# A fixed order on TensorE for both attentions of an encoder layer: the second turned and multiplied in pairs of key chunks, the first with other places for scores and v tiles

## The chip, the cores and the metric

The kernel runs on one core of one Trainium2 chip. A core has a matrix engine (TensorE, PE in the profile; its weight loads are PEld), three engines for element-wise work (VectorE or DVE, ScalarE or ACT, GpSimd or POOL), a queue engine that issues most transfers (SyncE or SP), on-chip memory (SBUF), accumulation banks that PE writes (PSUM), and 16 DMA engines. Each engine runs its own instructions in order, and engines wait for each other through semaphores. The metric is the device time of one execution in microseconds, as the median of several runs.

## The reference

One layer of a bidirectional encoder over 2048 tokens of 1024 features, batch 1, all float32:

```python
h  = rms_norm(x, norm_mix[l])
z  = h @ w_in[l]             # q_A k_A v_A q_B k_B v_B gate_A gate_B
y_a = windowed_gqa(q_a, k_a, v_a, sink[l])        # |t-s| <= 128, ALiBi, 8 heads, 2 kv heads
y_b = neighborhood_attn(q_b, k_b, v_b, rpb[l])    # 8 heads, 32 x 64 grid, 8 x 16 neighbours
gates = sigmoid([g_a, g_b] + b_gate[l])
x  = x + (gates_a * (y_a @ w_proj_a[l]) + gates_b * (y_b @ w_proj_b[l])) @ w_out[l]
x  = x + square(relu(rms_norm(x) @ w_up[l])) @ w_down[l]
return rms_norm(x, norm_final)
```

The first attention (A) lets each token see the tokens within 128 places, with a linear bias by distance and a sink logit for each head. The second (B) puts the tokens on a grid of 32 rows by 64 columns; each sees a window of 8 rows by 16 columns, with a learned bias for each head and offset. Heads are 64 wide.

## The kernel before, in words

**Precision.** A large product is made of three matmuls of float32r halves (lines 203 to 205 of a helper `mm3`: high by high, high by low, low by high). An attention product uses two (probabilities split into a high part `ph` and a low part `pl`).

**Stages.** Input projections of the first token pages as block products (0 to 358 us of the span); attention A (358 to about 627); attention B (to about 1022); gates, projections and merge (to about 1340); the MLP's two products (to the end). Both attentions need little of PE and much of the other engines, so the rest of the input projection, "feature" tiles, is laid between their matmuls. `dense` lists these tiles: q, k and v of A and B, and 16 gate tiles, each for two pages of 512 tokens. `feature_steps` does one tile in 8 steps of three 512-column matmuls into a PSUM bank "mm" (two of them) and yields after each; `fill = chain(dense)` strings the tiles together. Weights of a tile arrive by DMA (`raw`), ACT rounds them (`whl`, L179, about 1 us) and DVE or POOL takes the low part (L180, 2.4 us on POOL). ACT and DVE take a finished tile out of "mm". A v tile is then transposed: ACT copies it to `z` (L737), PE turns that copy by four transposes (`v_parts`, L423), and ACT and DVE take the result out.

**Attention A.** 32 units of 128 query tokens by one kv head (4 query heads). `Unit.load` fetches the queries (qraw), `order` arranges them on POOL (qa, L797). `score(u)` makes one quarter's scores (two matmuls, L815) into one of three "s" banks; DVE adds the bias and takes the row maximum in the same instruction (`sa`, L819). After the fourth quarter comes the softmax: four exps on ACT (L826), sums and reciprocal on DVE (L827, L828), four scalings on POOL (L830). `turn(c)` transposes one chunk of 128 keys by four transposes (L837) into one of two "pt" banks, ACT copies it as `ph` (L841), DVE makes `pl` (L842). `product(c)` multiplies both by the values into the one "av" bank (L852, L853); after the unit's last chunk ACT copies one half out (`ya`, L859) and DVE adds the other (L860), and the sum goes to memory `y_a` over SP.

The order on PE is written out by hand here: under `in_turn()` each group is put behind the last one issued (`issued[0]`). For each of a unit's chunks (3; 2 at the ends of the sequence): the turn, scores of the unit three ahead (quarters 0, then 1 and 2, then 3 in the three chunks), feature steps by `plain(upto)`, which spreads 24 tiles (one page each) of 8 steps evenly over the chunks, and the product of the chunk before. Ahead of this loop the first three units' scores are given without a fixed order, and 20 feature steps with one.

**Attention B.** 32 units of 8 heads by 4 column bands (`attn_b`). Each fetches its queries (`qb`, three buffers) and values (`vb`), makes four score blocks (L1038; 288 to 512 columns) that DVE reduces with the unit's bias (`sb`, L1043), does the softmax (exps L1049 on ACT, L1051 on DVE, L1054 on POOL), and then, for four pairs of key chunks, transposes into "pt" (L1066), copies (`phb` L1071, `plb` L1072) and multiplies into "av" (L1078); at the end ACT and DVE take the sum out (`yb`, L1086, L1087). Bias tables are made on POOL (L1006) from a fetched table (`braw`, L1000) for 22 of the 32 units. Keys of a head (`kb`, 2 MB in three DMAs, L1015 to L1017) have two buffers. What PE does when is not written out here: the scheduler places a unit's instructions, `drive` gives units two ahead, and `paced` puts each remaining feature tile behind the last product of some unit (`done`), 20 tiles of the 44 left in one call and 24 in another.

**Queues.** Transfers share SP's queue in order; a transfer into memory that attention A used must wait until the last reader there is done.

Of the kernel before, what the change touches and what calls it, by code (L numbers as in the profile page):

```python
# [19 lines left out]
BH = 8  # L20
# [75 lines left out]
def encoder_layer(ctx, tc, x, norm_mix, w_in, b_gate, sink, rpb, w_pa, w_pb, w_out,  # L96
# [323 lines left out]
    def v_parts(col, b, vt, p2, v2):  # L420

        for t in range(4):
            PE.transpose(p2[:, t * P : (t + 1) * P], vt[:, t * P : (t + 1) * P], ident)  # L423
# [304 lines left out]
    def v_tile(col):  # L728
        raw = load_slice([(cols(w_in[0], col), KC)])
        yield  # L730
        hl = split_slice(raw, V if col == O_VA else G)
        yield
        for b in (2, 3):
            ps = psum("mm", 2)
            yield from feature_steps(ps, hl, hp[b])
            vt = T(wp, [P, 2, BT], F32, "z", 3)[:, 0]
            A.copy(vt, ps)  # L737
# [19 lines left out]
        G.tensor_scalar(t, t, slope[:, g : g + 1], 1.0, ALU.mult, ALU.mult)  # L757
        bias_a[g] = t

    done, began, shares = [], [], []  # L760
# [19 lines left out]
    def in_turn():  # L780
        return tc.issue_after(issued[0]) if issued[0] else nullcontext()
# [89 lines left out]
                next(gens[k + 1])  # L871
            yield from g

    def drive(units, live, last, ahead=2):

        for u in units:
            next(u)
            live.append(u)
            if len(live) > ahead:
                next(live.pop(0), None)  # L880
        while last and live:
            next(live.pop(0), None)

    def paced(filler, pieces, total, lag):

        for n in pieces:
            at = min(n * 32 // total - lag, 31)
            with tc.issue_after(done[at]) if at >= 0 else nullcontext():
                piece(filler)

    def piece(filler):
        while next(filler, None):
            pass

    def gate_tile(f, blocks):
        raw = load_slice([(cols(w_in[0], O_GA + f * P), KC)])
        yield
# [43 lines left out]
    given = 0  # L941

    def plain(upto):
        nonlocal given
        while given < upto:
            with in_turn():
                next(fill)
            given += 1

    plain(FIRST)  # L950
# [24 lines left out]
    flush(queue=SY)  # L975
    s_a.close()

# [39 lines left out]
        SY.dma_start(k[64:128, 1].bitcast(F32), kd[0:64])  # L1017
        return k

    def attn_b(n_u, h, j, k, bias):  # L1020
        e, t = h % 2, h // 2
        w, jt = B_W[j], JT[j]
        kp = 4 * w
        q = T(bp, [P, 4, P], F32R, f"qb{n_u % 3}", 1)
        SY.dma_start(q.bitcast(F32), qs_b[t][e][:, :, j])
        yield
        v = T(bp, [P, 8, P], F32R, f"vb{n_u % 3}", 1)
        SY.dma_start(v[: 4 * w].rearrange("p (b c) d -> p b (c d)", b=4).bitcast(F32),
                     vs_b[t][4 * B_C0[j] : 4 * (B_C0[j] + w), :, e * 256 : e * 256 + 256])
        st = T(bp, [P, 4, 4], F32, "stb", 8)  # L1030
        mx, nm, sm, ri = (st[:, n, :] for n in range(4))
        kv = k.rearrange("p z (q f) -> p z q f", q=8)
        s = []
        for i in range(4):
            n = B_NR[i] * w
            ps = psum("s", 3)
            for z in range(2):
                PE.matmul(ps[:, :n], q[:, i, :],  # L1038
                          kv[:, z, B_R0[i] // 4 : (B_R0[i] + B_NR[i]) // 4, 4 * B_C0[j] : 4 * (B_C0[j] + w)],
                          start=z == 0, stop=z == 1)  # L1040
            o = boff[(jt, IT[i])]
            si = T(bp, [P, 512], F32, f"sb{n_u % 3}", 4)
            V.tensor_tensor_reduce(out=si[:, :n], in0=ps[:, :n], in1=bias[:, o : o + n], scale=1.0, scalar=-3.0e38,  # L1043
                                   op0=ALU.add, op1=ALU.max, accum_out=mx[:, i : i + 1])
            s.append(si)
        A.activation(nm, mx, AF.Copy, scale=-0.125)
        for i in range(4):
            n = B_NR[i] * w
            last_exp[0] = A.activation(s[i][:, :n], s[i][:, :n], AF.Exp, bias=nm[:, i : i + 1], scale=0.125,  # L1049
                                       accum_out=sm[:, i : i + 1]).ins  # L1050
        V.reciprocal(ri, sm)  # L1051
        for i in range(4):
            n = B_NR[i] * w
            G.tensor_scalar(s[i][:, :n], s[i][:, :n], ri[:, i : i + 1], 1.0, ALU.mult, ALU.mult)  # L1054
        yield
        flush(queue=SY)
        po = psum("av", 1)
        first = True
        for pair in range(4):
            pt = psum("pt", 2)  # L1060
            at, pieces = 0, []
            for c in (2 * pair, 2 * pair + 1):
                i0, ni = B_USE[c]
                for i in range(i0, i0 + ni):
                    rr = (4 * c - B_R0[i]) * w
                    PE.transpose(pt[:kp, at + (i - i0) * P : at + (i - i0 + 1) * P], s[i][:, rr : rr + kp], ident)  # L1066
                pieces.append((c, i0, ni, at))
                at += ni * P
            ph = T(bp, [P, 512], F32R, "phb", 3)
            pl = T(bp, [P, 512], F32R, "plb", 3)  # L1070
            last_parts[0] = (A.copy(ph[:kp, :at], pt[:kp, :at]).ins,  # L1071
                             V.tensor_tensor(out=pl[:kp, :at], in0=pt[:kp, :at], in1=ph[:kp, :at].bitcast(F32),  # L1072
                                             op=ALU.subtract).ins)
            if pair == 0:
                pieces.reverse()
            for c, i0, ni, o in pieces:
                for z, src in enumerate((ph, pl)):
                    last = PE.matmul(po[:, i0 * P : (i0 + ni) * P], v[:kp, c, :],  # L1078
                              src[:kp, o : o + ni * P], start=first, stop=(c == 7 and z == 1),
                              skip_group_check=True).ins  # L1080
                    first = False
        done.append(last)

        at = n_u % 2 * 64
        y = yb[at : at + 64]
        A.copy(y, po[64 - at : 128 - at, :])  # L1086
        V.tensor_tensor(out=y, in0=po[at : at + 64, :], in1=y, op=ALU.add)  # L1087
        put(y_b[t].rearrange("(e d) (i j t) -> e d i j t", e=2, i=4, j=4)[e, :, :, j, :],
            y.rearrange("d (i t) -> d i t", i=4))

    def all_b():
        for h in range(BH):
            k = load_k(h)

            for n, j in enumerate((0, 3, 1, 2) if h == 0 else range(4)):
                if j != 2:
                    bias = make_bias_b(h, JT[j])
                u = attn_b(4 * h + n, h, j, k, bias)
                next(u)
                yield u  # L1100

    def ahead_of(units, n):
        ready = []
        for u in units:
            ready.append(u)
            if len(ready) > n:
                yield ready.pop(0)
        yield from ready
# [5 lines left out]
    flush(queue=SY)  # L1114
    drive(units, live, True)
    flush(queue=SY)
    s_b.close()
    s_pg = ExitStack()
# [25 lines left out]

    first_y = load_y(0)
    first_load = last_dma[0]
    paced(fill, range(20, 44), 38, 4)
    s_h.close()


# [596 lines left out]
```

## Time and profile before

| what | value |
|---|---|
| median of three runs | 2611.38 us (2610.45 to 2614.44) |
| the profiled execution's own time | 2610.25 us |
| its span, first to last instruction | 2608.4 us |
| PE busy between 336 and 358 us | 21.17 of 22.00 us |
| PE busy between 1022 and 1300 us | 278.00 of 278.00 us |
| mean granted clock of PE | 0.998 |

The span leaves out 1.85 us around the first and last instruction. A row of a timeline gives the start and the length of a group of like instructions, its engine, line, operation and tiles (out<-in), and in brackets the idle time ahead of it with what ended it. Matmuls are pipelined: a printed length of 0.39 us for a 512-column matmul holds some 0.16 of overlap with the next, so the distance between starts is what a matmul costs. Granted clock is the share of full speed at which PE was allowed to run.

### The profile page before, as it was taken

How to read it: one execution, taken by the hardware profiler on the slowest of the kernel's cores; microseconds unless marked ns; L12 is line 12 of the kernel's file. 1: busy time of each engine (PE TensorE's matmuls, PEld its weight loads, DVE VectorE, ACT ScalarE, POOL GpSimd, SP SyncE). 2: the span in 40 equal slices, each digit the busy share in tenths (PEclk: the TensorE clock that was granted, in tenths of full speed). 3: DMA queues.
4: the chain of work that ended last, by engine and by line, in shares of the span. 5: the costliest groups of instructions: out<-in, count | busy, mean ns of one | idle time of the engine just before them, and what ended most of it. 6: DMA issues, size and time to landing. Idle time of an engine off the chain costs nothing.

```text
span 2608.4 us, 34594 instructions
## 1 busy us (share of the span) xinstructions
PE 2572.6 (99%) x12140; PEld 2144.1 (82%) x12140; DVE 1610.4 (62%) x2621; ACT 1233.2 (47%) x2261; POOL 367.0 (14%) x493
## 2 busy tenths in 40 slices
PE   8999999999999999999999999999999999999999
PEld 6888878878888888888888888888888888888887
DVE  9866566665434444765478777766656535554766
ACT  5335347666545555543335544644444332323454
POOL 1000124454545541000000000100000000000010
PEclk9999999999999999999999999999999999999999
DMA  5657485467875745865465765854428825445555
GB/s 185 203 156 204 135 263 155 125 169 194 216 188 171 202 141 180 281 198 159 153 202 198 242 217 199 309 179 146 158 97 310 294 97 186 146 146 169 185 192 172
DMA packets 354127, 490.40 MB, mean 188 GB/s; under 512 B 28808, under 2 KB 188808, under 8 KB 351776
## 3 DMA queue, kind: packets, MB, share of 16 engines
q1 hardware_dynamic: 346896, 471.14, 57.8%
q10 hardware_dynamic: 7056, 17.04, 1.8%
q8 instruction: 96, 1.57, 0.3%
q14 instruction: 79, 0.65, 0.1%
HBM read 328.64 MB, written 159.45 MB: 187 GB/s over the span
## 4 chain that ended last, share of the span: by engine, by line
PE 90%; DVE 3%; DMA 3%; ACT 2%; issue 1%; SPq 0%; POOL 0%; POOLq 0%; DVEq 0%; ACTq 0%
PE b L311 15%; PE b L312 15%; PE b L313 15%; PE mm L203 6%; PE mm L205 6%; PE mm L204 6%; PE zb L313 3%; PE zb L311 3%; PE zb L312 3%; PE pt L203 2%; PE pt L204 2%; PE pt L205 2%; PE av L1078 2%; PE pt L1066 2%; PE s L1038 2%; PE pt L837 1%
## 5 line engine op out<-in xcount | busy, mean ns | idle before, releaser
L312 PE MATMUL b<-dwh,dah 128*128 128x512 f32 x896 | 348.6, 389 | 0.0
L313 PE MATMUL b<-dwh,dah 128*128 128x512 f32 x896 | 347.6, 389 | 0.0
L311 PE MATMUL b<-dwh,dah 128*128 128x512 f32 x896 | 339.6, 389 | 0.0
L307 ACT CAST dah<-da 128x1024 fp32r<-128x1024 f32 (+1 forms) x128 | 120.8, 945 | 368.8 <-PE b L313 240.5
L308 DVE TENSOR_TENSOR dah<-da,dah 128x1024 fp32r<-128x1024 f32 (+1 forms) x128 | 139.4, 1089 | 222.3 <-ACT dah L307 222.1
L312 PE MATMUL b<-ubh,uwhlb 128*128 128x512 f32 x592 | 230.3, 389 | 0.0
L311 PE MATMUL b<-ubh,uwhlb 128*128 128x512 f32 x592 | 230.3, 389 | 0.0
L313 PE MATMUL b<-ubh,uwhlb 128*128 128x512 f32 x592 | 229.2, 389 | 0.0
L203 PE MATMUL mm<-hT,whl 128*128 128x512 f32 x544 | 218.2, 401 | 0.0
L205 PE MATMUL mm<-hT,whl 128*128 128x512 f32 x544 | 215.1, 395 | 0.0
L204 PE MATMUL mm<-hT,whl 128*128 128x512 f32 x544 | 214.8, 395 | 0.0
L311 PEld LDWEIGHTS b<-dwh,dah 128*128 128x128 f32 x896 | 168.2, 188 | 34.9
L313 PEld LDWEIGHTS b<-dwh,dah 128*128 128x128 f32 x896 | 168.2, 188 | 34.9
L312 PEld LDWEIGHTS b<-dwh,dah 128*128 128x128 f32 x896 | 168.2, 188 | 34.8
L311 PE MATMUL zb<-zh,zwhl 128*128 128x512 f32 x476 | 186.4, 394 | 6.6 <-DVE st L251 1.6
L312 PE MATMUL zb<-zh,zwhl 128*128 128x512 f32 x476 | 186.3, 391 | 0.0
L313 PE MATMUL zb<-zh,zwhl 128*128 128x512 f32 x476 | 183.9, 392 | 0.3 <-DVE zwhl L308 0.3
L302 DVE TENSOR_TENSOR uc<-b,uc 128x512 f32<-128x512 f32 x160 | 108.9, 687 | 104.6 <-PE b L313 103.5
L1617 POOL TENSOR_TENSOR st<-st,power 128x1 f32<-128x1 f32 x16 | 13.3, 841 | 925.2 <-DVE st L1616 925.2
L311 PEld LDWEIGHTS b<-ubh,uwhlb 128*128 128x128 f32 x592 | 111.2, 188 | 23.4 <-issue 0.4
L312 PEld LDWEIGHTS b<-ubh,uwhlb 128*128 128x128 f32 x592 | 111.2, 188 | 23.1
L313 PEld LDWEIGHTS b<-ubh,uwhlb 128*128 128x128 f32 x592 | 111.1, 188 | 23.1
(255 smaller groups left out, 5840.0 us busy)
## 6 DMA issues: line engine op xcount, KB each, us to landing
at<-uc SPq DMA_DIRECT2D x224, 256.0 KB
da<-at SPq DMA_DIRECT2D x96, 512.0 KB
dw<-in_w_down_dram SPq DMA_DIRECT2D x160, 256.0 KB
uraw<-in_w_up_dram SPq DMA_DIRECT2D x32, 1024.0 KB
raw<-in_w_in_dram SPq DMA_DIRECT2D x34, 512.0 KB
zraw<-in_w_in_dram SPq DMA_DIRECT2D x16, 1024.0 KB
z<-zg SPq DMA_DIRECT2D x64, 256.0 KB
zg<-zc SPq DMA_DIRECT2D x32, 256.0 KB
```

The costliest lines, as they stand in the source:

```text
L203: PE.matmul(ps, lh, rh, start=first, stop=False)
L204: PE.matmul(ps, lh, rl, start=False, stop=False)
L205: return PE.matmul(ps, ll, rh, start=False, stop=last).ins
L302: return eng.tensor_tensor(out=out, in0=a, in1=b, op=op).ins
L307: casts.append(A.copy(hi, src).ins)
L308: return eng.tensor_tensor(out=lo, in0=src, in1=hi.bitcast(F32), op=ALU.subtract).ins
L311: PE.matmul(ps, lh, rh, start=first, stop=False, skip_group_check=True)
L312: PE.matmul(ps, lh, rl, start=False, stop=False, skip_group_check=True)
L313: PE.matmul(ps, ll, rh, start=False, stop=last, skip_group_check=True)
L1038: PE.matmul(ps[:, :n], q[:, i, :], kv[:, z, B_R0[i] // 4 : (B_R0[i] + B_NR[i]) // 4, 4 * B_C0[j] : 4 * (B_C0[j] + w)], start=z == 0, stop= ...
L1066: PE.transpose(pt[:kp, at + (i - i0) * P : at + (i - i0 + 1) * P], s[i][:, rr : rr + kp], ident)
L1078: last = PE.matmul(po[:, i0 * P : (i0 + ni) * P], v[:kp, c, :], src[:kp, o : o + ni * P], start=first, stop=(c == 7 and z == 1), skip_grou ...
```

## The change

Both attentions now run on PE in an order that the program fixes. Numbers of matmuls and their shapes stay the same on PE.

In A, the first three units' scores stand at set feature steps (`FIRST`: ahead of quarter 3 of unit 0 are 12 steps, and so on to 21), in order from that quarter on. The scores three units ahead are given as quarters 0 and 1, 2 and 3, none in a unit's three chunks. `plain` gets its numbers from weights (a score 0.27, a step 0.68) so that scores and steps together are even. A v tile yields "turn" after its copy, and its transposes are an owed step of their own, given ahead of the next feature step.

```diff
         for t in range(4):
-            PE.transpose(p2[:, t * P : (t + 1) * P], vt[:, t * P : (t + 1) * P], ident)
+            issued[0] = PE.transpose(p2[:, t * P : (t + 1) * P], vt[:, t * P : (t + 1) * P], ident).ins
         if col == O_VA:
...
+            yield "turn"
             out = v_parts(col, b, vt, psum("mm", 2), T(wp, [P, 2, BT], F32, "z", 3).rearrange("p a b -> p (a b)"))
             for dst, t in out:
                 SY.dma_start(dst, t)
@@ -757,7 +758,7 @@
...
-    AHEAD, FIRST, PLAIN = 3, 20, 24 * KC
+    AHEAD, PLAIN, SCORE, STEP = 3, 24 * KC, 0.27, 0.68
+    FIRST = {(0, 3): 12, (1, 2): 14, (2, 0): 16, (2, 2): 18, (3, 0): 21}
...
+    given, owed = 0, [False]
+
+    def plain(upto):
+        nonlocal given
+        while given < upto:
+            if owed[0]:
+                with in_turn():
+                    next(fill)
+            with in_turn():
+                owed[0] = next(fill) == "turn"
+            given += 1
 
...
     for n in range(AHEAD):
         prepare(n)
         for u in range(4):
-            units[n].score(u, False)
...
+                plain(FIRST[n, u])
+            units[n].score(u, (n, u) >= (0, 3))
+    plain(FIRST[AHEAD, 0])
     chunks = [(n, c) for n, x in enumerate(units) for c in range(x.c0, x.c1)]
-    behind = []
+    behind, scored, begin = [], 0, given
+    whole = (PLAIN - given) * STEP + 4 * (len(units) - AHEAD) * SCORE
...
         if n + AHEAD < len(units):
-            for u in {0: (0, 1), 1: (2, 3)}[c - x.c0] if x.c1 - x.c0 == 2 else {0: (0,), 1: (1, 2), 2: (3,)}[c]:
+            for u in {0: (0, 1), 1: (2, 3)}[c - x.c0] if x.c1 - x.c0 == 2 else {0: (0, 1), 1: (2, 3), 2: ()}[c]:
                 units[n + AHEAD].score(u)
-        plain(FIRST + (at + 1) * (PLAIN - FIRST) // len(chunks))
+                scored += 1
+        plain(begin + round(((at + 1) / len(chunks) * whole - scored * SCORE) / STEP))
         if len(behind) > 1:
             y, *z = behind.pop(0)
             y.product(*z)
     y, *z = behind.pop(0)
     y.product(*z)
-    live = []
-    issued[0] = None
-    del done[:]
+    if owed[0]:
+        next(fill)
+        owed[0] = False
```

In B the generator `attn_b` with `drive`, `paced` and `all_b` gives way to a class `Near` with `load`, `load_v`, `score`, `turn` and `product`, whose bodies hold the same instructions under `in_turn()`. The loop goes by pairs of key chunks: the turn of a pair, one score block of the unit two ahead, feature steps by the same kind of weights (a score 0.4), the product of the pair before. A tile counts once for each of its two pages, 68 in all: 24 are given in A as before, 41 in B, and three behind it.

```diff
...
+    class Near:
...
+        def turn(self, pair):
+            w, kp = self.w, 4 * self.w
...
+            with in_turn():
+                for c in (2 * pair, 2 * pair + 1):
...
-    units = ahead_of(all_b(), 1)
-    drive((next(units) for _ in range(15)), live, False)
-    paced(fill, range(20), 38, 4)
-    flush(queue=SY)
-    drive(units, live, True)
...
+    units = [Near(4 * h + n, h, j) for h in range(BH) for n, j in enumerate((0, 3, 1, 2) if h == 0 else range(4))]
+    kbs, bias = {0: load_k(0)}, None
+    for n in range(2):
+        bias = units[n].load(bias)
+    for n in range(2):
+        units[n].load_v()
+        for i in range(4):
+            units[n].score(i, False)
+        if n == 0:
+            kbs[1] = load_k(1)
+            bias = units[2].load(bias)
+    pairs = [(n, p) for n in range(len(units)) for p in range(4)]
+    scored, begin, SCORE, last_plain = 0, given, 0.4, 41 * KC
+    whole = (last_plain + PLAIN - given) * STEP + 4 * (len(units) - 2) * SCORE
+    for at, (n, p) in enumerate(pairs):
+        x = units[n]
+        if p == 0:
+            if n % 4 == 2 and n + 6 < len(units):
+                kbs[(n + 6) // 4] = load_k((n + 6) // 4)
+            if n + 3 < len(units):
+                bias = units[n + 3].load(bias)
+        if p == 1 and n + 2 < len(units):
+            units[n + 2].load_v()
+        behind.append((x, p, *x.turn(p)))
+        if n + 2 < len(units):
+            units[n + 2].score(p)
+            scored += 1
+        plain(begin + round(((at + 1) / len(pairs) * whole - scored * SCORE) / STEP))
+        if len(behind) > 1:
+            y, *z = behind.pop(0)
+            y.product(*z)
+    y, *z = behind.pop(0)
+    y.product(*z)
     flush(queue=SY)
...
-    paced(fill, range(20, 44), 38, 4)
+    for _ in fill:
+        pass
```

The start of A on PE, up to the first turn (pt). `s` tiles are scores, `mm` tiles feature steps; `qa_3047` is unit 0's, `s` on it its last quarter. Before:

```order
L815 MATMUL s_3066<-ka_292_2963,qa_3047 128x256 x2
L815 MATMUL s_3087<-ka_292_2963,qa_3051 128x288 x2
L815 MATMUL s_3091<-ka_292_2963,qa_3051 128x288 x2
L203 MATMUL mm_3215<-hT_2921,whl_3029 128x512
...
L205 MATMUL mm_3215<-hT_2921,whl_3029 128x512
L815 MATMUL s_3095<-ka_292_2963,qa_3051 128x288 x2
L815 MATMUL s_3099<-ka_292_2963,qa_3051 128x288 x2
L815 MATMUL s_3120<-ka_292_2963,qa_3084 128x288 x2
L815 MATMUL s_3124<-ka_292_2963,qa_3084 128x288 x2
L815 MATMUL s_3128<-ka_292_2963,qa_3084 128x288 x2
L815 MATMUL s_3132<-ka_292_2963,qa_3084 128x288 x2
L837 MATMUL pt_3232<-ident,sa_2966 128x128 x4
```

After:

```order
L816 MATMUL s_3111<-ka_292_2963,qa_3047 128x256 x2
L816 MATMUL s_3132<-ka_292_2963,qa_3051 128x288 x2
L816 MATMUL s_3136<-ka_292_2963,qa_3051 128x288 x2
...
L205 MATMUL mm_3098<-hT_3015,whl_2996 128x512
L816 MATMUL s_3146<-ka_292_2963,qa_3051 128x288 x2
L816 MATMUL s_3150<-ka_292_2963,qa_3051 128x288 x2
...
L816 MATMUL s_3202<-ka_292_2963,qa_3129 128x288 x2
L816 MATMUL s_3206<-ka_292_2963,qa_3129 128x288 x2
L203 MATMUL mm_3195<-hT_2921,whl_3029 128x512
...
L204 MATMUL mm_3195<-hT_2936,whl_3029 128x512
L205 MATMUL mm_3195<-hT_2935,whl_3029 128x512
L838 MATMUL pt_3235<-ident,sa_2966 128x128 x4
```

Twelve feature matmuls and 16 score matmuls stood between unit 0's last score and the first turn; now it is 27 and 16, with the scores in pairs between the steps.

In the middle of A on PE, the boundary between two units' sums in the "av" bank. Before:

```order
L852 MATMUL av_3461<-ph_3469,va_294_2965 128x512
L853 MATMUL av_3461<-pl_3470,va_294_2965 128x512
L837 MATMUL pt_3524<-ident,sa_2969 128x128 x4
L815 MATMUL s_3533<-ka_292_2963,qa_3393 128x288 x2
L815 MATMUL s_3537<-ka_292_2963,qa_3393 128x288 x2
L203 MATMUL mm_3457<-hT_2935,whl_3212 128x512
...
L205 MATMUL mm_3457<-hT_2935,whl_3212 128x512
L852 MATMUL av_3547<-ph_3503,va_294_2965 128x512
L853 MATMUL av_3547<-pl_3504,va_294_2965 128x512
```

After, with a v tile's transposes (L423) that stand some rows ahead of the same boundary:

```order
L204 MATMUL mm_3327<-hT_3016,whl_3029 128x512
L205 MATMUL mm_3327<-hT_3015,whl_3029 128x512
L423 MATMUL mm_3459<-ident,z_3457 128x128 x4
...
L853 MATMUL av_3477<-ph_3485,va_294_2965 128x512
L854 MATMUL av_3477<-pl_3486,va_294_2965 128x512
L838 MATMUL pt_3531<-ident,sa_2969 128x128 x4
L816 MATMUL s_3540<-ka_292_2963,qa_3396 128x288 x2
L816 MATMUL s_3544<-ka_292_2963,qa_3396 128x288 x2
L203 MATMUL mm_3473<-hT_2935,whl_3192 128x512
...
L205 MATMUL mm_3473<-hT_2935,whl_3192 128x512
L853 MATMUL av_3563<-ph_3506,va_294_2965 128x512
L854 MATMUL av_3563<-pl_3507,va_294_2965 128x512
```

Between the last product of one unit (av_3461, now av_3477) and the first of the next there were six feature matmuls and now there are three. The transposes stand right behind the last matmul of their own tile.

From A to B on PE. `av` on `va` is A's product; `pt` on `sb` a turn of B; `kb` with `qb_695` (before) or `qb_696` (after) are the scores of B's third unit. Before:

```order
L853 MATMUL av_6089<-pl_6068,va_294_2965 128x512
L1066 MATMUL pt_6321<-ident,sb_689_6205 96x128
L1066 MATMUL pt_6321<-ident,sb_690_6210 96x128 x2
L1066 MATMUL pt_6321<-ident,sb_691_6215 96x128
L423 MATMUL mm_6079<-ident,z_6077 128x128 x4
L203 MATMUL mm_7500<-hT_2921,whl_5910 128x512
...
L203 MATMUL mm_7500<-hT_2935,whl_5910 128x512
L1066 MATMUL pt_6334<-ident,sb_690_6210 96x128
L1066 MATMUL pt_6334<-ident,sb_691_6215 96x128 x2
L1078 MATMUL av_6308<-phb_6313,vb_687_6199 128x256
L1078 MATMUL av_6308<-plb_6314,vb_687_6199 128x256
L1038 MATMUL s_6278<-kb_680_6179,qb_695_6238 128x384 x2
```

After:

```order
L853 MATMUL av_6079<-ph_6067,va_294_2965 128x512
L854 MATMUL av_6079<-pl_6068,va_294_2965 128x512
L423 MATMUL mm_6088<-ident,z_6077 128x128 x4
L1068 MATMUL pt_6279<-ident,sb_689_6205 96x128 x2
L1068 MATMUL pt_6279<-ident,sb_690_6210 96x128
L1037 MATMUL s_6288<-kb_680_6179,qb_696_6242 128x384 x2
L203 MATMUL mm_6298<-hT_2921,whl_5936 128x512
...
L205 MATMUL mm_6298<-hT_2921,whl_5936 128x512
L1068 MATMUL pt_6310<-ident,sb_689_6205 96x128
L1068 MATMUL pt_6310<-ident,sb_690_6210 96x128 x2
L1068 MATMUL pt_6310<-ident,sb_691_6215 96x128
L1037 MATMUL s_6319<-kb_680_6179,qb_696_6242 128x512 x2
```

Between A's last product and the third unit's first score stood 22 feature matmuls, four v transposes, two turns and two products of B; now four v transposes and one turn of three stand there.

More of the change, by code (lines that the diff above doesn't have):

```diff
@@ L1035, in attn_b @@
             n = B_NR[i] * w
             ps = psum("s", 3)
[L1037 to L1043, printed above, removed]
+            with in_turn() if forced else nullcontext():
+                for z in range(2):
+                    ins = PE.matmul(ps[:, :n], self.q[:, i, :],
+                                    kv[:, z, B_R0[i] // 4 : (B_R0[i] + B_NR[i]) // 4, 4 * B_C0[j] : 4 * (B_C0[j] + w)],
+                                    start=z == 0, stop=z == 1).ins
@@ L1044, in attn_b @@
+            if forced:
+                issued[0] = ins
+            o = boff[(self.jt, IT[i])]
+            si = T(bp, [P, 512], F32, f"sb{self.n % 3}", 4)
+            V.tensor_tensor_reduce(out=si[:, :n], in0=ps[:, :n], in1=self.bias[:, o : o + n], scale=1.0, scalar=-3.0e38,
                                    op0=ALU.add, op1=ALU.max, accum_out=mx[:, i : i + 1])
             s.append(si)
[L1046 to L1055, printed above, removed]
-        flush(queue=SY)
-        po = psum("av", 1)
-        first = True
-        for pair in range(4):
+            if i < 3:
+                return
+            A.activation(nm, mx, AF.Copy, scale=-0.125)
+            for i in range(4):
+                n = B_NR[i] * w
+                last_exp[0] = A.activation(s[i][:, :n], s[i][:, :n], AF.Exp, bias=nm[:, i : i + 1], scale=0.125,
+                                           accum_out=sm[:, i : i + 1]).ins
@@ L1073, in attn_b, with product @@
                                              op=ALU.subtract).ins)
+            return ph, pl, pieces
+        def product(self, pair, ph, pl, pieces):
+            kp = 4 * self.w
             if pair == 0:
+                self.po = psum("av", 1)
                 pieces.reverse()
[L1076 to L1108, printed above, removed]
-    units = ahead_of(all_b(), 1)
-    drive((next(units) for _ in range(15)), live, False)
-    paced(fill, range(20), 38, 4)
-    flush(queue=SY)
-    drive(units, live, True)
+            po = self.po
+            with in_turn():
+                for x, (c, i0, ni, o) in enumerate(pieces):
+                    for z, src in enumerate((ph, pl)):
+                        ins = PE.matmul(po[:, i0 * P : (i0 + ni) * P], self.v[:kp, c, :], src[:kp, o : o + ni * P],
+                                        start=pair == x == z == 0, stop=(c == 7 and z == 1), skip_group_check=True).ins
```

92 lines of the change are left out of this document (45 added, 47 removed).

## The prediction

> **What bounds the kernel now.** I read the page's busy table and the shares of its chain first, then TensorE's waits, then the busy time by stage.
>
> ```profile
> PE 2572.6 (99%) x12140; PEld 2144.1 (82%) x12140; DVE 1610.4 (62%) x2621; ACT 1233.2 (47%) x2261; POOL 367.0 (14%) x493
> PE 90%; DVE 3%; DMA 3%; ACT 2%; issue 1%; SPq 0%; POOL 0%; POOLq 0%; DVEq 0%; ACTq 0%
> ...
> PE mm L423 <- ACT z L737: 3.8, 4, 1.5
> PE s L1038 <- DMA kb<-ks_b: 3.7, 1, 3.7
> PE av L852 <- DVE ya L860: 3.4, 5, 1.4
> ...
> PE s L1038 <- DVE stb L1043: 0.7, 3, 0.3
> ...
> 358.00:609.00 251.00, 242.83 (x1330) 202.83 (x1329) 161.39 (x463) 167.27 (x472) 111.17 (x189) 0.99 0.61 165
> 609.00:1022.00 413.00, 407.73 (x2322) 354.05 (x2321) 185.09 (x468) 225.75 (x535) 199.53 (x217) 1.00 0.66 182
> ```
>
> TensorE (PE) is busy 99% of the span, and the chain that ends last is 90% PE. The waits are printed as total, times, longest. The two attentions lie between 358 and 1022 us, and of these 664 us PE lacks 8.2 in the first window and 5.3 in the second. As the change leaves PE the same matmuls (it only sets their order), its gain is bounded by these 13.5 us, plus what half clock costs; its loss has no such bound.
>
> Half clock is the part that the waits do not print:
>
> ```profile
> 374.60:378.00 3.40, 2.62 (x11) 1.45 (x11) 2.68 (x13) 2.54 (x12) 2.24 (x6) 1.00 1.05 382
> 378.00:381.40 3.40, 3.40 (x14) 3.00 (x15) 2.57 (x9) 2.76 (x12) 2.31 (x5) 0.50 1.17 313
> ...
> 643.90:647.60 3.70, 0.30 (x2) 0.00 (x0) 1.11 (x4) 2.92 (x9) 0.73 (x2) 1.00 1.06 234
> 647.70:651.00 3.30, 3.14 (x8) 2.59 (x9) 0.56 (x3) 0.39 (x1) 1.83 (x2) 0.50 1.08 355
> ```
>
> The third column from the right is PE's granted clock. Twice a stretch with idle time is followed by some 3.4 us at 0.50, which does 1.7 us of work: a stall here has a price of its own length plus 1.7.
>
> **Start of the first attention.** PE's timeline, and POOL's one row at the place:
>
> ```profile
> 369.84 0.93 PE L815 MATMUL s<-ka,qa 128*128 128x256 f32 x6
> ...
> 373.61 1.57 PE L815 MATMUL s<-ka,qa 128*128 128x288 f32 x8
> 375.48 0.97 PE L815 MATMUL s<-ka,qa 128*128 128x288 f32 x4 [0.30 <-DVE sta L819]
> 376.59 1.68 PE L837 MATMUL pt<-ident,sa 128*128 128x128 f32 x4
> 377.95 1.27 PE L815 MATMUL s<-ka,qa 128*128 128x288 f32 x4
> ...
> 376.13 1.68 POOL L830 TENSOR_SCALAR sa<-sa,sta 128x160 f32<-128x160 f32 x4 [1.16 <-DVE sta L828]
> ```
>
> The row at 369.84 holds unit 0's last score; its softmax ends on POOL at 377.81, 7.7 us after that score (0.24 us for its two matmuls of 256). The turn (pt) at 376.59 needs it. The prices for PE work, start to start, come from the timeline rows in the next part: 0.23 us for a feature matmul of 512 columns, 0.13 for a score matmul of 288 (about 0.15 there), 0.09 to 0.11 for a transpose. In the order before, 16 score matmuls and 12 feature matmuls stand between that score and the turn: 2.1 + 2.7 = 4.9 us, 2.9 less than the softmax took. From 373.61 to 378.0 PE did 12 score matmuls and 4 transposes, 2.0 us of work in 4.4: 2.4 lost, and 1.7 at half clock, 4.1 in all. In the new order 16 score matmuls and 27 feature matmuls stand there: 2.1 + 6.2 = 8.3 us, more than 7.7. The stall and its half clock go: **-4.1**. The cover is thin (0.6 us); if it fails by 1 us, half clock comes back and about 2.7 of the 4.1 is lost again.
>
> **v tiles.** L423's transposes wait for ACT's copy of the feature tile (3.8 us in four waits, above). The new "turn" step is to put other work between. In the new order, though, four of the six v tiles of this stage still have their transposes straight behind the tile's last feature matmul (one is shown in the part on the change): the pacing asks for two steps at once there, and the owed step follows without a score or product between. One has 1.4 us between, one 0.9. Four before, four after: **0**, with bounds of -3.8 (all hidden) and +0.5.
>
> **The one av bank.** A unit's first product waits until the last unit's sum has been taken out of PSUM by ACT (L859) and DVE (L860).
>
> ```profile
> L859 ACT COPY ya<-av x32: 582/584/586, 388.1 to 627.4; 64x512 f32<-64x512 f32 x32
> ...
> L860 DVE TENSOR_TENSOR ya<-av,ya x32: 671/682/684, 388.7 to 628.0; 64x512 f32<-64x512 f32 x32
> ...
> 582.99 0.39 PE L853 MATMUL av<-pl,va 128*128 128x512 f32 x1
> 583.22 0.60 PE L837 MATMUL pt<-ident,sa 128*128 128x128 f32 x4
> 583.57 0.77 PE L815 MATMUL s<-ka,qa 128*128 128x288 f32 x4
> 584.17 0.39 PE L203 MATMUL mm<-hT,whl 128*128 128x512 f32 x1
> 584.40 0.40 PE L204 MATMUL mm<-hT,whl 128*128 128x512 f32 x1
> ...
> 586.44 0.50 PE L852 MATMUL av<-ph,va 128*128 128x512 f32 x1 [1.41 <-DVE ya L860]
> ...
> 582.91 1.06 ACT L179 CAST whl<-raw 128x1024 fp32r<-128x1024 f32 x1
> ```
>
> Copy and add take 0.58 + 0.68, and with about 0.1 of hand-over 1.4 us. The place at 583 has four transposes, four score matmuls and three feature matmuls between two units, 1.66 us by my prices; that is enough where nothing is ahead on ACT and DVE, and 1.4 too little where a cast (1.06) is ahead of the copy. Most gaps before hold six feature matmuls (2.35). Counted over the whole stage, 5 of 31 gaps are 1.66 before and 15 of 31 after. Of the 31 take-outs in this trace 19 took 1.4 us, and 12 between 1.6 and 3.1. A gap of 1.66 would lose 0.28 us in the mean by this distribution, one of 2.35 0.08: 15 x 0.28 + 16 x 0.08 = 5.5 us, against 5 x 0.28 + 26 x 0.08 = 3.5 for the old order, which the 3.4 of the waits confirms. That is +2.0; some of the new gaps have lighter DVE work ahead, so I take **+1.2**, between 0 and +10 (every 1.66 gap behind a cast, 15 x 0.9 less 3.4).
>
> **From the first attention to the second.** SP's queue and PE's timeline here:
>
> ```profile
> 626.47 0.61 SPq L1000 DMA_DIRECT2D braw<-tab  x1
> 627.21 0.56 SPq L1025 DMA_DIRECT2D qb<-qs_b  x1
> 633.47 0.34 SPq L1015 DMA_DIRECT2D kb<-ks_b  x1
> ...
> 626.28 0.40 PE L853 MATMUL av<-pl,va 128*128 128x512 f32 x1
> ...
> 632.97 1.46 PE L1038 MATMUL s<-kb,qb 128*128 128x384 f32 x6
> ...
> 643.90 0.29 PE L1038 MATMUL s<-kb,qb 128*128 128x288 f32 x1
> 647.86 0.58 PE L1038 MATMUL s<-kb,qb 128*128 128x288 f32 x1 [3.66 <-DMA kb<-ks_b]
> ```
>
> The first attention ends on PE at 626.68. Before, PE waits 3.66 us for the second head's keys (kb), issued at 633.47, needed 17.2 us after that end and landed 21.1 after it; with half clock 5.4. In the new order 23.9 us of PE work stand ahead of that use, so this wait goes.
>
> Another comes. The q tile of unit 2 (qb2) lies in memory that the first attention's last product reads, so its DMA can be issued only after that product: 627.21, 0.53 after the end, as in the order before. Then its first reader (632.97) stood behind some twenty feature matmuls. Now it is PE's third piece of work, behind four v transposes and three of the first turn: 0.6 us after the end. PE is in order, so everything behind stands. How long depends on the landing. No view prints it; by the packet records it was 5.5 us after the issue here (632.73, consistent with the reader's 632.97), and over all 32 q loads between 2.9 and well over 5, with a median of 4.0. The stall is 0.53 + 5.5 - 0.6 = 5.4 us for the same landing, 2.8 for the fastest. I take 5.0, nearest to the same transfer in the same traffic, and 1.7 of half clock: 6.7 against 5.4, **+1.3**, between -2.6 (2.8, no half clock) and +3.4 (5.4 and two windows). braw, issued ahead, feeds POOL's bias for the same unit, which would be ready at about the landing too; it adds nothing beyond 0.5.
>
> [...]
>
> **The second attention.** Its steady state, from the groups between 609 and 1022:
>
> ```profile
> L1049 ACT ACTIVATE sb<-sb,stb 128x384 f32<-128x384 f32 x64 | 38.8, 607 | 1.1
> L1466 ACT ACTIVATE z<-z,bg 128x512 f32<-128x512 f32 x4 | 2.7, 716 | 0.0
> L1466 ACT ACT_TABLE_LOAD x1 | 1.3, 1283 | 0.0
> L180 POOL TENSOR_TENSOR whl<-raw,whl 128x1024 fp32r<-128x1024 f32 x22 | 52.8, 2400 | 56.7 <-ACT whl L179 53.3 <-PE pt L1066 3.4
> L1054 POOL TENSOR_SCALAR sb<-sb,stb 128x384 f32<-128x384 f32 x64 | 37.2, 590 | 43.6 <-DVE stb L1051 37.5 <-PE s L1038 6.0
> L1006 POOL TENSOR_TENSOR biasl<-braw,masks 128x512 f32<-128x512 f32 x8 | 12.6, 1570 | 0.0
> ```
>
> Now a unit's last score stands 13.2 us of PE work or more ahead of its first turn (24 and more before). The softmax between, undisturbed, is about 5.9 us (reduce, four exps of some 0.6, reciprocal, four POOL scalings of 0.59). POOL may put a weight split (2.4) and three bias tiles (about 4.0 with the 1.57 one) ahead: 12.3, which fits by 0.9. Turn to product is 4.5 us or more, against 0.6 + 0.6 for its two copies. The small waits of this stage (stb 0.7, and shorter ones not attributed) had to do with uneven order; I take **-0.9**, bounds -2 and +9 (the rival below).
>
> At its end the table load and four sigmoids (1.3 + 4 x 0.72 = 4.2 us on ACT) now sit ahead of the last copies that a product waits for. Before, they hid behind feature matmuls; I put **+1.2**, bounds 0 and 2.5. The three remaining blocks of features after it change no total.
>
> **Sum.** -4.1 + 0 + 1.2 + 1.3 - 0.9 + 1.2 = -1.3. The profiled execution took 2610.25 us (span 2608.4), 1.13 under the median of 2611.38. So 2609.0 on its scale, 2610.1 as a median.
>
> **Rivals.** (1) The q tile lands quickly: 2.9 us, no half clock, so the seam gives -2.6; and as order is even the av bank costs no more than before (0). -4.1 - 2.6 - 0.9 = -7.6: 2603.8. For it: the median landing of 4.0; against it: the same DMA in the same traffic took 5.5, and a stall of 2.8 is longer than the 0.8 of idle time that was followed by half clock at 378. [...]
>
> (2) POOL is late in the second attention. Its slack is 0.9 us; a bias load or a DVE queue 1.3 us late uses it up, and the order then stops PE at the first turn, where the old order, forced less and 24 us ahead, had room. Some 22 units make a bias; 22 x 0.4 = +8.8 on the sum: 2618.9. For it: kb loads of 2 MB took 14 us and hold up small ones; against: POOL is busy only 199.53 of 413 us. 0.15.
>
> (3) The av bank: casts of 1.06 ahead of the copy at nearly all 15 short gaps, +10 in place of +1.2: also 2618.9. It decides from about ten such places on; before, five of 31 take-outs began over 0.7 us late. 0.07.
>
> (4) The "turn" works better than I count: -3.8 more, 2606.3. It is inside the forecast's range.
>
> **Numbers.** The forecast has 0.49: 2610.1, by its own bounds 2606 to 2615. Measurement tells about 0.2% (5.2 us) from no change, that is under 2606.2 or over 2616.6. Faster 0.29 (case 1), same 0.49, slower 0.22 (2 and 3). The range of 2602.5 to 2619.5 takes in the three rivals' times.
>
> **What would show it.** Right: no half clock near 378; no kb wait; one wait at unit 2's first score, releaser qb, 4 to 6 us, with 3.4 us at half clock behind; 3 to 4 waits at L423; the ya waits at 4 to 7 us in 8 to 15 times. Wrong: a wait for sb or POOL at the turns of the second attention (case 2), no qb wait (case 1), or half clock at more than two places.

## The result and the profile after

The change makes the kernel slightly slower: 2614.89 us against 2611.56 (medians of 20 runs each), a ratio of 1.0013 with a 95% interval of 1.0007 to 1.0020. The forecast was 2610.1, 1.3 us faster. The measured 3.3 us lie within the range (2602.5 to 2619.5) and within 0.2% of no change, but on the other side.

The profiled execution of the change took 2616.45 us (span 2614.0), 1.6 above its median; that of before lay 1.3 under its own. So the two profiles differ by 5.6 us of span, more than the medians do, and what follows explains those 5.6.

TensorE's waits in the changed kernel (total, times, longest):

```profile
PE mm L423 <- ACT z L737: 5.8, 5, 1.7
PE av L853 <- DVE ya L861: 4.1, 6, 0.8
PE s L1037 <- DMA qb<-qs_b: 4.0, 1, 4.0
PE av L1089 <- DVE yb L1098: 3.5, 2, 3.2
...
PE s L816 <- DVE sta L820: 1.7, 1, 1.7
...
PE av L854 <- DVE pl L843: 0.4, 2, 0.2
```

The wait for kb (3.7) is gone, and the one for qb has come, as forecast. One row was not in the sum, 1.7 us of a score waiting for DVE; another, 3.2 of a product waiting for yb, stood in it at 1.2. The row of L423 has grown by 2.0.

The windows by stage, in the form shown of before:

```profile
358.00:609.00 251.00, 241.36 (x1330) 201.81 (x1329) 160.72 (x467) 165.53 (x475) 113.59 (x191) 0.99 0.62 165
609.00:1022.00 413.00, 402.84 (x2301) 351.99 (x2300) 187.49 (x467) 229.71 (x535) 197.75 (x215) 0.99 0.68 183
```

PE is busy 1.5 us less in the first and 4.9 less in the second. A matmul at half clock counts as busy (3.41 of 3.41 us between 633.48 and 636.89, at a granted clock of 0.50), so half clock is not in these. To count both, I summed, over successive PE starts in a stretch of the trace, the distance between starts less what the matmul costs at full clock (0.228 us for 512 columns, 0.176 for 384, 0.132 for 288, 0.109 for a transpose, and so on, as these traces have the distances where PE waits for nothing). This is PE time lost, in us:

| stretch | before | change | bias early | sigmoids late | fill at seam | v apart | four edits | two av banks |
|---|---|---|---|---|---|---|---|---|
| 340-400, start of A | 7.6 | 7.1 | 2.6 | 7.8 | 4.8 | 3.5 | 2.6 | 2.2 |
| 400-620, A | 10.1 | 12.1 | 11.9 | 12.1 | 12.0 | 9.0 | 9.1 | 7.6 |
| 620-660, A to B | 5.9 | 6.4 | 6.6 | 6.6 | 0.6 | 7.3 | 0.6 | 0.7 |
| 660-980, B | 10.4 | 9.6 | 9.6 | 9.6 | 14.0 | 9.5 | 10.7 | 8.7 |
| 980-1020, end of B | 2.5 | 5.7 | 4.2 | 0.8 | 5.1 | 5.7 | 0.5 | 0.4 |

The last six columns are the experiments below. Before to change: -0.5, +2.0, +0.5, -0.8, +3.2, together +4.4; the rest of the 5.6 lies outside these stretches. Of it PE's busy time between 1022 and 1300 us shows 0.5 (278.00 before, 277.50 now).

**The start of A.** DVE's, POOL's, SP's and PE's timelines of the changed kernel:

```profile
365.33 0.57 SPq L757 DMA_DIRECT2D biasa<-in_dist_a_dram  x1
...
368.61 0.51 POOL L758 TENSOR_SCALAR biasa<-biasa,byhead 128x288 f32<-128x288 f32 x1 [8.35 <-DMA biasa<-in_dist_a_dram]
...
369.15 0.38 DVE L820 CUSTOM_DVE_ANT_0 sa<-s,biasa,byhead 128x160 f32<-128x160 f32 x1 [9.41 <-POOL biasa L758]
...
367.50 0.39 PE L205 MATMUL mm<-hT,whl 128*128 128x512 f32 x1
369.60 1.29 PE L816 MATMUL s<-ka,qa 128*128 128x256 f32 x6 [1.71 <-DVE sta L820]
370.69 0.63 PE L203 MATMUL mm<-hT,whl 128*128 128x512 f32 x1
...
380.05 0.60 PE L838 MATMUL pt<-ident,sa 128*128 128x128 f32 x4
```

The score is unit 0's last, now fixed at feature step 12. Three score banks hold the unit's first three quarters, DVE empties a bank while it adds the bias table (biasa), and that table's transfer leaves SP's queue only at 365.33. PE reaches the score 1.7 us before a bank comes free. The feature matmul behind the scores prints 0.63 in place of 0.39: half clock (granted 0.50 from 370.65 to 374.07). The first turn (380.05) has no wait. Half clock stretched its distance from the score to 10.4 us here; in the early-bias kernel below, without half clock, 8.7 us were enough too, near the 8.3 of the forecast.

The table was as late in the kernel before, as DVE's timeline there shows:

```profile
368.98 0.38 DVE L819 CUSTOM_DVE_ANT_0 sa<-s,biasa,byhead 128x160 f32<-128x160 f32 x1 [9.85 <-POOL biasa L757]
```

There PE came to the score only at 369.84, after 16 feature steps (48 matmuls); in the new order it comes after 12.

**The end of B.** ACT and PE:

```profile
993.67 1.28 ACT L1486 ACT_TABLE_LOAD   x1
994.97 2.56 ACT L1486 ACTIVATE z<-z,bg 128x512 f32<-128x512 f32 x4
997.43 0.46 ACT L1075 CAST phb<-pt 128x384 fp32r<-128x384 f32 x1
997.79 0.58 ACT L884 COPY z<-mm 128x512 f32<-128x512 f32 x1
998.27 1.05 ACT L179 CAST whl<-raw 128x1024 fp32r<-128x1024 f32 x1
...
999.34 0.58 ACT L1097 COPY yb<-av 64x512 f32<-64x512 f32 x1
...
1000.70 0.39 PE L1089 MATMUL av<-phb,vb 128*128 128x256 f32 x1 [3.16 <-DVE yb L1098]
```

Table load and sigmoids hold ACT for 3.8 us; a copy, a drain and a weight cast that came due meanwhile stand behind them, and the copy of the sum last. PE waits 3.2 us, and half clock follows (granted 0.50 from 1002.12 to 1005.53).

### The profile page after: what moved, and what is told of

Same layout as the page of the kernel before. It is cut to its first block, busy times and chain, and to the rows that moved or that the text cites. A ratio compares the mean times of both kernels' runs of the same rounds, so it can differ in the third digit from the quotient of the medians.

```text
span 2614.0 us, 34536 instructions
## 1 busy us (share of the span) xinstructions
PE 2571.5 (98%) x12140; PEld 2145.5 (82%) x12140; DVE 1608.9 (62%) x2621; ACT 1233.6 (47%) x2261; POOL 366.1 (14%) x493
## 4 chain that ended last, share of the span: by engine, by line
PE 90%; DMA 3%; DVE 3%; ACT 2%; issue 1%; SPq 1%; POOL 0%; POOLq 0%; DVEq 0%; ACTq 0%
PE b L311 15%; PE b L312 15%; PE b L313 15%; PE mm L203 5%; PE mm L205 5%; PE mm L204 5%; PE zb L311 3%; PE zb L313 3%; PE zb L312 3%; PE pt L203 2%; PE pt L204 2%; PE pt L205 2%; PE av L1089 2%; PE pt L1068 2%; PE s L1037 2%; PE pt L838 1%
```

## Experiments

Each kernel but one (the first attention alone) is the changed one with the edit shown. Each is timed against the kernel before in five rounds; ratios are to that kernel, so 1.0013 is the change itself.

**The bias table's transfer.**

```diff
-        SY.dma_start(t, dist_a)
+        (A if g == 1 else SY).dma_start(t, dist_a)
```

> The changed kernel, with one edit: the load of the first attention's first bias table is issued from ACT's queue, where it stands behind work that ends at 356, and not from SP's, where it was issued at 365.33. PE's order is the same row for row. Theory: PE's wait of 1.7 us at 367.5 (unit 0's last score, for a score bank) was a wait for this table, as DVE cannot empty a score bank without it; it falls to 0, the stretch at half clock behind it (370.7 to 373) goes too, and about 3.4 us are gained: about 2611.5. Rival: the bank is late for another reason (queries, or the fixed place itself), the wait stays and the time stays at about 2614.9.

1.0003 (0.9995 to 1.0011). DVE and PE at the place:

```profile
366.91 0.38 DVE L820 CUSTOM_DVE_ANT_0 sa<-s,biasa,byhead 128x160 f32<-128x160 f32 x1 [7.35 <-POOL biasa L758]
...
367.56 1.04 PE L816 MATMUL s<-ka,qa 128*128 128x256 f32 x6
```

ACT's queue issued it at 362.61, not at 356, still early enough: DVE starts 2.2 us sooner, the score waits for nothing, no half clock follows, and the stretch loses 2.6 in place of 7.1. The wait was for this table. Of the 4.5 us, some 3.5 lie between 366 and 384 us; 0.8 is a wait at 347, ahead of A, that differs from trace to trace and is not the edit's. By the ratios the gain is 0.10%, 2.6 us; the intervals overlap, so the time alone would not show it, and the trace does. (The 4.2 at the end of B in its column is the same 3.2 us wait without half clock behind it.)

**The sigmoids.** A reference to the last ACT copy of B's sum is kept as `last_y`.

```diff
-            with tc.issue_after(last_exp[0]):
+            with tc.issue_after(last_y[0]):
                 A.activation(g, g, AF.Sigmoid, bias=bg[:, 8 * n + f : 8 * n + f + 1])
```

> The changed kernel, with one edit: the merge's first sigmoids (and the table load that goes with them) are held behind the last copy of the second attention's sum on ACT, instead of behind its last exp. Theory: at 997.15 PE waited 3.2 us for that sum because 1.3 + 2.6 us of table load and sigmoids stood ahead of the copies on ACT; the wait and the half clock behind it (1002 to 1005) go, 4.5 us or so: about 2610.4. The merge's first product is 20 us away and covers the table load. Rival: the load only moves on, into the merge, where DVE then waits for the sigmoid and PE for a bank: gain under 1.5 us, with a new wait near 1036.

0.9997 (0.9989 to 1.0005), 0.16% or 4.2 us under the change. The end of B in both, PE busy first:

```profile
980.00:1020.00 40.00, 36.84 (x203) 31.77 (x202) 11.96 (x27) 21.21 (x43) 9.35 (x10) 0.96 0.48 145
```

```profile
980.00:1020.00 40.00, 40.00 (x228) 34.95 (x227) 16.21 (x34) 21.57 (x46) 9.36 (x10) 1.00 0.56 162
```

Above the change, below this kernel: idle time and half clock are gone (busy 40.00 of 40.00 us, granted 1.00), and none of PE's waits in this run is put down to the table load or the sigmoids where they now stand.

**Fill between the attentions.**

```diff
+    plain(given + 8)
     scored, begin, SCORE, last_plain = 0, given, 0.4, 41 * KC
```

> The changed kernel, with one edit: 8 feature steps (24 matmuls, 5.5 us) are given between the first attention's last product and the second's first turn; the rest of the steps are spread over the second attention as before. Theory: the wait of 4.0 us for unit 2's query tile and the half clock behind it are covered, and 5.5 to 5.9 us are gained: about 2609.2. Rival: the second attention is now short of 8 steps and something else ends last at the seam (the bias table of the same unit, or the second head's keys): a new wait of 1 to 4 us shows at the seam, and the gain is 2 us or less.

1.0013 (1.0004 to 1.0021): nothing gained. The seam lost 0.6 us in place of 6.4, so the qb wait and its half clock did go. But B lost 14.0 in place of 9.6, and its waits say why:

```profile
PE mm L423 <- ACT z L737: 9.2, 7, 2.9
...
PE av L1089 <- DVE yb L1098: 3.4, 4, 2.5
```

Eight steps less to spread shift which of B's pairs gets how many, and three v tiles of B now have their transposes straight behind their own last matmul. The worst on PE and ACT:

```profile
737.70 0.39 PE L205 MATMUL mm<-hT,whl 128*128 128x512 f32 x1
741.00 0.66 PE L423 MATMUL mm<-ident,z 128*128 128x128 f32 x4 [2.91 <-ACT z L737]
...
737.76 0.62 ACT L1052 ACTIVATE sb<-sb,stb 128x384 f32<-128x384 f32 x1
...
740.39 0.56 ACT L737 COPY z<-mm 128x512 f32<-128x512 f32 x1
```

The four exps of a unit stand ahead of the copy. Neither side had this one: the rival's size was right, its place (the seam) wrong.

**v transposes apart.**

```diff
                 owed[0] = next(fill) == "turn"
             given += 1
+            if owed[0]:
+                return
```

> The changed kernel, with one edit: when a v tile yields its turn, the call that gives feature steps returns, so that the owed transposes come after the next product, turn and scores (1.1 to 1.4 us of PE work) and never right behind their tile. Theory: the four waits of the first attention at L423 (0.8, 1.9, 1.2, 0.8 us beyond the matmul's own time) came from their place, and fall to under 0.3 each: 4 us gained, about 2610.9; the fifth one, at 682 in the second attention, where the transposes already stood apart, stays. Rival: ACT is late itself (exps or casts ahead of the copy), and half of the waits stay: gain under 2 us.

0.9999 (0.9990 to 1.0007), 3.7 us under the change; the two intervals just touch.

```profile
PE mm L423 <- ACT z L737: 1.7, 2, 1.4
...
PE s L816 <- DVE sta L820: 1.4, 1, 1.4
```

5.8 has become 1.7, and what is left is mostly the fifth wait, in B (1.4). The place was the cause in A. The score's wait, untouched, was not followed by half clock this time (granted 1.00 from 364.40 to 374.64; see the last section), so the 3.5 in the first stretch of its column, against 7.1, is not all the edit's: the old wait that ended at 398 (0.8) is, half clock is not.

**The first attention alone**, with B as before:

> The kernel before with the change's part for the first attention alone; the second attention is placed by the scheduler as before. Theory: the first attention's part costs 1.5 us by itself (start -0.5, steady +2.0), so about 2613 and a ratio of 1.0005, with the old wait for the second head's keys (3.7 us) still there; the rest of the change's +0.13% lies behind 620 us. Rival: the first attention's part is the gain and the second's the whole loss: ratio under 0.9995.

1.0005 (0.9996 to 1.0014). It does not tell from no change; A's stretches lost 7.3 and 12.1, like the change's, and the seam showed the old kb wait (3.6). Nothing supports A's part as a gain.

**A's old scores and even pacing.**

```diff
-            for u in {0: (0, 1), 1: (2, 3)}[c - x.c0] if x.c1 - x.c0 == 2 else {0: (0, 1), 1: (2, 3), 2: ()}[c]:
+            for u in {0: (0, 1), 1: (2, 3)}[c - x.c0] if x.c1 - x.c0 == 2 else {0: (0,), 1: (1, 2), 2: (3,)}[c]:
...
-        plain(begin + round(((at + 1) / len(chunks) * whole - scored * SCORE) / STEP))
+        plain(begin + (at + 1) * (PLAIN - begin) // len(chunks))
```

> The changed kernel with one part undone: in the first attention the scores three units ahead stand in the three chunks as 1, 2 and 1 again, and the feature steps are spread evenly by count. Gaps of 1.66 us between two units' sums fall from 15 to 4 of 31, and one of six v tiles has its transposes behind its own tile, not four. Theory: the new scores and weights are what cost the first attention its 2 us more than before: the waits for ya (4.1 us) fall to 1 to 2 and those at L423 by 2 to 3: 4 to 6 us under the changed kernel, about 2610. Rival: scores and pacing are neutral, the 2 us come from v tiles alone: 2 us gained or less, with the ya waits still at 3 to 4.

1.0008 (1.0000 to 1.0017): 1.3 us under the change, which the overlapping intervals do not tell from nothing.

```profile
PE s L1037 <- DMA qb<-qs_b: 5.7, 1, 5.7
PE av L853 <- DVE ya L861: 4.5, 8, 1.3
PE mm L423 <- ACT z L737: 3.5, 3, 1.6
```

With 4 short gaps in place of 15 the ya waits are not smaller but slightly larger, 4.5 for 4.1. The rival holds: for the ya waits scores and weights are neutral, and what this kernel gained is v tiles (5.8 to 3.5), part of which the qb wait took back. The weights do matter for the v tiles, as they decide which of them have their transposes straight behind.

**All four edits together.**

> The changed kernel with the four edits of the first set together (bias load from ACT's queue, sigmoids behind the last copy, 8 feature steps between the attentions, v transposes apart). Theory: the four waits are separate, PE is the bound in between, and what each edit takes out adds up: 2 to 4 us (bias), 4 to 5 (sigmoids), 5.8 (seam; what that edit lost again in the second attention were v tiles whose transposes fell behind their own tile, which the fourth edit now keeps apart), 3 to 4 (v tiles). 15 to 18 us under the changed kernel: 2597 to 2600, ratio to the kernel before about 0.995. Rival: a fixed order hands a removed stall on to the next late partner (as the fill at the seam did), and half or more comes back in the second attention: 2604 to 2608.

2599.04 us, 0.9953 (0.9940 to 0.9965), 0.60% under the change and 0.47% under the kernel before. By the ratios it is 15.7 us faster than the change, and the profile's span is 17.8 us shorter; 15 to 18 were expected. By the table, the seam and the end of B are near nothing, A's start is at 2.6, and most of the cost that the fill alone brought into B is gone (10.7). PE's waits that remain in the attentions:

```profile
PE av L853 <- DVE ya L861: 4.3, 6, 0.8
PE mm L423 <- ACT z L737: 2.2, 2, 1.8
...
PE av L1091 <- DVE yb L1100: 0.9, 3, 0.4
PE av L854 <- DVE pl L843: 0.7, 3, 0.3
```

The same with A's old scores and pacing:

> The four edits together, and the old scores and even pacing of the first attention. Theory: on top of the four edits the ya waits fall by 2 to 3 us; v tiles are already apart there, so no more from them: 2594 to 2598, ratio about 0.994, the fastest of all. Rival: with the stalls gone elsewhere the short gaps are covered by DVE and ACT being less late, and it equals the four edits within 1 us.

0.9960 (0.9946 to 0.9973): no better, ya at 4.5 us again, as the reading above asks.

**Two av banks.** In the four-edit kernel `psum("av", 1)` becomes 2 and `psum("s", 3)` becomes 2, in the merge's use of both names too.

> The four edits together, with two 'av' banks and two 's' banks, where they have one and three (PSUM is full). Theory: with a second av bank the first product of a unit no longer waits for the last sum's way out, so the waits for ya (4.3 us in six) and yb (0.9) go to 0; what two score banks cost is new: a unit's scores come in pairs, and a score then waits for DVE if DVE is over about 0.7 us behind, which its longest queue there (a reduce of 0.5, a subtraction of 0.7) makes about as often as it made ya late. Within 3 us of the four edits either way, 2596 to 2602; the ya row gone, a row of s waiting for sta in its place. Rival: the score banks are not needed (the third one idles): a gain of the whole 5 us, about 2594.

2594.67 us, 0.9941 (0.9928 to 0.9955): the lowest ratio of the study, though its interval overlaps that of the four edits.

```profile
PE mm L423 <- ACT z L737: 3.0, 3, 1.8
PE av L854 <- DVE pl L843: 3.0, 3, 2.6
...
PE s L816 <- DVE sta L820: 0.4, 1, 0.4
```

The rows of ya and yb are gone, and a third score bank would have saved some 0.4 us, by the last row. A wait of 2.6 for pl came in their place, so 3.3 of the 5 us show in the span. One small DVE sum stood before it:

```profile
561.57 4.64 DVE L828 TENSOR_TENSOR sta<-sta 128x4 f32<-128x4 f32 x1 [1.94 <-ACT sa L827]
```

In the median this sum takes 0.16 us. POOL worked here without a gap from 560.30 to 566.20, and the sum ended at 566.21. So it was with all 19 of these sums that took over 0.3 us in the eleven traces: each overlapped work of POOL and ended within 0.03 us of the end of one of POOL's instructions. That the sum is held until POOL is done is my reading of these ends; no run here takes POOL's work away to show it.

## Why the prediction was wrong, step by step

- **Start of A, -4.1 forecast, about -0.5 measured.** "The stall and its half clock go" was the step that failed. The turn's stall did go. What was not asked is what the moved score needs: four steps (12 feature matmuls) earlier, it came before the bias table could empty a bank for it. The trace of before had that row (DVE idle until 368.98, shown above); I priced the distance from the score to the turn and not from the table to the score. So a new stall of 1.7 us came with half clock of its own, and between 366 and 384 us PE lost 3.8 us, against 4.2 before. Moving one DMA to another queue took the new stall away with PE's order unchanged.
- **v tiles, 0 forecast.** Right in A: four waits before and after, 4.5 and 4.8 us of lost time. The changed kernel's fifth wait, in B at 682 (1.7 us, behind exps on ACT), was left out of the sum. That adjacency was the cause in A is shown by the v-apart kernel.
- **The av bank, +1.2 forecast, +0.7 measured** (3.4 to 4.1). The size was near, the reason was not: the waits do not follow the number of short gaps (4.5 us with 4 of them). In all six of the change casts or copies on ACT, or reduces and subtractions on DVE, stand ahead of the sum's way out. Two banks end them.
- **A to B, +1.3 forecast, +0.5 measured.** Mechanism right: kb gone, qb come, one half clock (granted 0.50 from 633.48 to 636.89). The stall was 4.0 where I took 5.0, as the tile landed 4.3 us after its issue and not 5.5.
- **B, -0.9 forecast, -0.8 measured**, though that holds the 1.7 of the v tile: by difference, the small waits fell by some 2.5. POOL's slack of 0.9 us held; no turn waited for sb.
- **End of B, +1.2 forecast, +3.2 measured**, above my bound of 2.5. The block of 4.2 us on ACT was seen and the wait undersized: I counted the block, and neither the copy, drain and cast that pile up behind it nor the half clock that followed.
- **The rivals.** None came about: qb did not land quickly (4.3 us, between the 2.9 of that case and the 5.5), POOL was not late, nearly all short gaps being late did not happen. The sum of the first, -7.6, leaves out the +1.2 of the end of B without a reason; with it the time would have been 2605.0. A sum of -1.3 out of terms with bounds of several us each said little of the sign; two terms, the start of A (3.6 off) and the end of B (2.0 off), decide it. That the time still fell into the range is due to the width of the range.

## What to carry to other kernels

When an instruction is moved earlier in a fixed order, ask of each of its operands, and of whatever must empty its output bank, when they are ready; the distance to its reader is half of the question. In this kernel a fixed order turned late partners into stalls of their own, and a fix in one place shifts counts elsewhere (the fill at the seam gained 5.8 us and lost 4.4): look at all the waits again after each edit, and mend them together. Where one engine serves short urgent copies and long work that can wait, hold the long work back behind the last urgent copy.

## What was not expected of the hardware

In the traces of this case half clock begins on a grid. Windows of 3.41 us laid on it in the changed kernel (the third column from the right is the granted clock):

```profile
367.24:370.65 3.41, 1.70 (x9) 1.13 (x8) 1.50 (x9) 0.00 (x0) 0.99 (x2) 1.00 0.98 244
370.65:374.07 3.42, 3.42 (x12) 2.84 (x11) 1.58 (x7) 2.20 (x10) 0.13 (x1) 0.50 1.08 256
633.48:636.89 3.41, 3.41 (x9) 2.65 (x9) 0.57 (x2) 0.00 (x0) 2.82 (x3) 0.50 0.85 253
1002.12:1005.53 3.41, 3.41 (x10) 2.72 (x9) 0.69 (x1) 0.51 (x2) 0.00 (x0) 0.50 0.69 185
544.73:548.14 3.41, 1.67 (x11) 1.19 (x10) 1.17 (x4) 2.98 (x10) 0.80 (x2) 1.00 1.08 317
548.14:551.55 3.41, 3.41 (x22) 2.93 (x21) 1.81 (x6) 1.17 (x2) 1.15 (x3) 1.00 0.18 40
```

The three starts, 370.653, 633.479 and 1002.118 by the clock records, lie 77.00 and 108.00 times 3.4133 us apart, and each stretch lasts 3.413 us by the same records. In the kernel before, the starts at 378.001 and 647.654 lie 79.00 times that apart, and those of the other kernels lie whole multiples apart in each of their traces. In the eleven traces every stall of 3.6 us or more in the two attentions brought one. The 3.2 at the end of B did in the change and did not in the kernel with the early bias; the 1.4 and 1.6 of the score's wait in the v-apart and the fill kernels brought none, the 1.7 of the change did. The window at 544.73, printed as idle as the one at 367.24 (1.67 and 1.70 of 3.41 busy), brought none either.

What does sort these windows is the matmul work in them, counted as in the table by what each matmul costs at full clock, so without the overlap that a printed length holds: 1.35 us in the one at 544.73, 1.23 in the one at 367.24. In the eleven traces 2175 windows of the grid lie between 350 and 1020 us. The 17 with half clock behind them held 1.27 us of work or less; of the others two held 1.27 as well and all the rest 1.28 or more. That the chip counts work in this way is not shown; the runs show the border.

An estimate from these numbers for this kernel: a stall of 2 or 3 us costs its own length, and 1.7 us more (half of 3.41) where it takes over 2.1 us of work (3.41 less 1.27) out of one window of the grid.
